# A projection of 512 tokens: one matmul of 512 columns into one PSUM bank instead of two of 256 into two

## The chip, the cores and the metric

The kernel runs on one core of one Trainium2 chip. The metric is the device time of one execution in microseconds; three executions of the kernel before took 2807.52, 2808.34 and 2809.0 us, so the median is 2808.34 us. The profile below is a fourth execution of the same program, recorded with the hardware profiler.

## The reference

The program computes two blocks one after the other on a sequence of 512 tokens with 1024 features, batch 1. The change lies in block 1, which has two layers of one form. Its 16 meta tokens are put ahead of the 512, so it works on 528. Everything is 32-bit.

```python
def hybrid_layer(x, ...):                       # block 1: run twice
    h = rms_norm(x, norm_g)
    z = h @ w_in
    aq, ak, av, ag, mq, mk, mv, mi, mf, mo, mgate = jnp.split(z, split_points(), axis=-1)
    q, k = rope(rms_norm(aq)), rope(rms_norm(ak))          # 16 query heads, 2 key heads of 64
    ya = sliding_window_sink_attention(q, k, av, sink) * silu(ag)
    mq, mk = silu(causal_depthwise_conv([mq, mk]))
    hm = rms_norm(mlstm_chunkwise(mq, mk, mv, mi, mf))     # 4 heads, value width 256
    ym = hm * sigmoid(mo) * silu(mgate)
    return x + jnp.concatenate([ya, ym], -1) @ w_out

def first_block(x, meta, ...):
    h = jnp.concatenate([meta, x], axis=1)
    for l in range(2):
        h = hybrid_layer(h, ...)
    return h[:, 16:]                            # the meta tokens' own output is dropped
```

Block 2 (differential, dilated and memory attention, two layers, then a norm) follows on the 512 tokens. As the meta rows are dropped at the end of block 1, its last layer needs queries (`aq`) and gates (`ag`, `mo`, `mgate`) for 512 tokens only; keys, values and the convolution inputs are needed for all 528.

## The kernel before

Activations lie with features on the 128 partitions and tokens along the free dimension. Every 32-bit operand is split into a rounded high part and a low part (`split`, L167: ScalarE casts the high part at L171, VectorE subtracts for the low part at L172), and each product is three matmuls: high times high, high times low, low times high. So a projection of 128 output features (`dense`, L195) is 24 matmuls over the eight feature tiles for each token range in `halves`, with a weight load ahead of every matmul. All matmuls are issued at L165. A weight chunk of 128x1024 comes by DMA and is itself split into `wh` and `wl` (`weights`, L177).

PSUM has two pools: `z` tiles of two banks, two of them, for the projections, and `a` tiles of one bank, four of them, for everything else. A projection in layer 0 covers 528 tokens as two ranges of 264 (`HALVES`), one in each bank of a `z` tile, and VectorE copies it out times the norm factor in one instruction (`evac1`, L352). In the last layer of block 1, 32 projections (8 of queries, 8 of attention gates, 16 of mLSTM gates) take the 512 tokens alone, as two ranges of 256 (`SEQ2`, chosen at L803 as `own`).

The layer's work is emitted in the order of `ORDER`: attention group 0, mLSTM head 0, attention group 1, and so on. Between projections, generators of the attention blocks (`a_block`, L462) and mLSTM heads (`m_head`, L651) are advanced by one step each (`step`, `round`). One attention block, for four heads and 128 queries, goes through the engines like this: TensorE computes two score tiles, VectorE adds the mask and takes the maximum of each head (L481), three small VectorE operations make the bias (L486 to L489), ScalarE takes four exponentials (L493), VectorE forms the sums and normalises (L497 to L501), TensorE transposes the result (L509), ScalarE and VectorE split it (L171, L172), and TensorE multiplies it with the values (L165, into an `a` tile of 128x4x112).

The order in which an engine's instructions finally stand is not that of the source: the program is laid out by a planner that runs it through its own estimate of durations, emits what is ready, and prefers older work, with the copies out of PSUM raised in rank (`high_priority`). Each engine then executes its list strictly in that order and waits on semaphores. So a change of one instruction's estimated duration moves others on all engines.

Of the kernel before, what the change touches and what calls it, by code (L numbers as in the profile page):

```python
# [13 lines left out]
ALU = mybir.AluOpType  # L14
# [5 lines left out]
L1 = 528  # L20
# [17 lines left out]
FULL = [(0, 512)]  # L38
HALVES = [(0, HB), (HB, L1)]
SEQ1 = [(16, L1)]  # L40
SEQ2 = [(16, 272), (272, L1)]


COL = {}
# [18 lines left out]
class Kernel:  # L63
# [281 lines left out]

    def evac1(self, ps, r, halves=HALVES):
        z = self.slot()
        (t, u), two = halves[0], lambda x: x[:, halves[0][0] :].rearrange("p (a b) -> p a b", a=2)
        if t:
            self.nc.vector.memset(z[:, :t], 0.0)  # L350
        with self.tc.high_priority(offset=AHEAD):
            self.nc.vector.tensor_tensor(two(z), ps[:, :, : u - t], two(r), ALU.mult)  # L352
        return z

    def qk_parts(self, z, gcol):
# [431 lines left out]
    def layer1(self, l, st, xsrc, nxt, first=()):  # L787

        nc, d = self.nc, self.d
        r = self.slot()  # L790
# [9 lines left out]
        self.release(raw)  # L800


        own = SEQ2 if l else HALVES  # L803

        def proj(halves=HALVES):
            ps = self.z()
# [67 lines left out]
        halves = HALVES if l == 0 else SEQ1  # L874
        acc = []
        for part, gens, y in ((0, attn, ya), (1, ml, yb)):
# [7 lines left out]
            for m in range(8):  # L884
                ps = self.z()
                outs = [ps[:, j, : b - a] for j, (a, b) in enumerate(halves)]
                self.dense(outs, [d["wo1"][l, m, part]], ys, halves)
                if part == 0:
                    x = self.slot()
# [720 lines left out]
```

## Time and profile before

| | |
|---|---|
| median of three executions | 2808.34 us (2807.52 to 2809.0) |
| the profiled execution: device time | 2809.2 us |
| the profiled execution: span of its instructions | 2807.4 us |
| TensorE (PE) busy | 2752.0 us, 98% |
| weight loads (PEld, beside PE) | 2439.8 us, 87% |
| VectorE (DVE) busy | 1627.0 us, 58% |
| ScalarE (ACT) busy | 1654.6 us, 59% |
| GpSimd (POOL) busy | 689.8 us, 25% |
| granted TensorE clock, mean | 0.995 |

Busy times are unions: instructions of one engine that overlap are counted once. Matmuls are pipelined, so the duration of a single matmul is longer than the distance from its start to that of the next; the time that a stream of matmuls takes is read from the starts. The span runs from the first to the last instruction; the device time of that execution is 1.8 us longer.

### The profile page before, as it was taken

Reading aid. Unit: us, or ns where it says so; the run is one execution under the profiler, and the core shown is the slowest. Engines: PE = TensorE matmul, PEld = TensorE weight load, DVE = VectorE, ACT = ScalarE, POOL = GpSimd, SP = SyncE. Lnnn points to the kernel's source line nnn. Section 1 sums busy time; section 2 is a strip of 40 time slices with the busy share of each in tenths; the row PEclk is TensorE's granted clock in tenths of the full one; section 3 lists DMA queues with packets and bytes.
Section 4 is the critical chain, followed back from the end, with each engine's and each line's share of the span. In section 5 each row is a group of like instructions: output and inputs, shape, how many; then the busy total and the mean of one; then the engine's idle time right before and its main releaser. Section 6 shows DMA issues by size and latency. Waiting matters only on the chain.

```text
span 2807.4 us, 44298 instructions
## 1 busy us (share of the span) xinstructions
PE 2752.0 (98%) x16806; PEld 2439.8 (87%) x16806; DVE 1627.0 (58%) x4079; ACT 1654.6 (59%) x2926; POOL 689.8 (25%) x790
## 2 busy tenths in 40 slices
PE   8999999999999999999999999999999999999998
PEld 7999999999999878888888888888888888888886
DVE  5788784478777545665445662344676452673333
ACT  6677775677777566777555442236777664553233
POOL 4233222313322322221111211222221121211231
PEclk9999999999999999999999999999999999999999
DMA  7655657766666886756766322347765777422332
GB/s 197 142 129 128 142 133 180 188 138 133 137 142 151 198 204 160 165 126 148 167 147 163 106 76 97 107 136 185 157 150 132 156 163 160 142 78 78 103 120 68
DMA packets 137668, 395.32 MB, mean 141 GB/s; under 512 B 14031, under 2 KB 40343, under 8 KB 137327
## 3 DMA queue, kind: packets, MB, share of 16 engines
q0 software_dynamic: 39456, 143.67, 30.7%
q1 hardware_dynamic: 96846, 247.77, 26.3%
q8 instruction: 132, 2.16, 0.3%
q10 hardware_dynamic: 1152, 1.05, 0.1%
q14 instruction: 82, 0.66, 0.1%
HBM read 383.85 MB, written 8.60 MB: 140 GB/s over the span
## 4 chain that ended last, share of the span: by engine, by line
PE 88%; ACT 6%; DVE 4%; issue 1%; DMA 0%; POOL 0%; DVEq 0%; SPq 0%; ACTq 0%
PE z L165 64%; PE a L165 20%; PE a L967 1%; PE a L509 1%; ACT s L1010 1%; ACT wl L186 1%; ACT wh L188 1%; DVE s L175 1%; DVE s L981 0%; ACT L1038 0%; ACT s L174 0%; DVE s L172 0%; ACT s L171 0%; ACT L229 0%; DMA s<-mem 0%
## 5 line engine op out<-in xcount | busy, mean ns | idle before, releaser
L165 PE MATMUL z<-s,wh 128*128 128x512 f32 (+2 forms) x6784 | 1263.4, 334 | 12.3 <-DVE s L175 3.4
L165 PEld LDWEIGHTS z<-s,wh 128*128 128x128 f32 x6784 | 1042.5, 189 | 143.2 <-DVE s L175 4.6
L165 PE MATMUL z<-s,wl 128*128 128x264 f32 (+2 forms) x3392 | 660.1, 333 | 0.0
L165 PEld LDWEIGHTS z<-s,wl 128*128 128x128 f32 x3392 | 525.7, 188 | 63.1 <-issue 0.5
L187 POOL DMA_DIRECT2D wl<-w x242 | 209.7, 867 | 1060.3 <-ACT wl L186 921.4
L188 ACT CAST wh<-wr 128x1024 fp32r<-128x1024 f32 x274 | 286.7, 1046 | 309.3 <-PE z L165 304.3
L165 PE MATMUL a<-s,s 128*128 128x512 f32 (+5 forms) x1900 | 420.9, 336 | 2.7 <-ACT s L171 1.7
L186 ACT ACTIVATE wl<-wr 128x1024 fp32r<-128x1024 f32 x274 | 288.4, 1056 | 86.3 <-PE z L165 82.9
L165 PEld LDWEIGHTS a<-s,s 128*128 128x128 f32 (+1 forms) x1900 | 295.4, 186 | 33.4 <-ACT s L171 3.3
L190 ACT CAST wh<-wr 128x1024 fp32r<-128x1024 f32 x130 | 136.2, 1049 | 278.3 <-PE z L165 168.7
L192 DVE TENSOR_TENSOR wl<-wr,wh 128x1024 fp32r<-128x1024 f32 x86 | 106.9, 1244 | 199.6 <-ACT wh L190 193.9
L165 PE MATMUL z<-wh,s 128*128 128x256 f32 x1408 | 208.9, 286 | 8.0 <-DVE s L175 7.7
L192 POOL TENSOR_TENSOR wl<-wr,wh 128x1024 fp32r<-128x1024 f32 x44 | 106.3, 2416 | 441.2 <-ACT wh L190 338.6
L172 DVE TENSOR_TENSOR s<-s,s 128x512 fp32r<-128x512 f32 (+7 forms) x266 | 183.8, 704 | 44.1 <-ACT s L171 37.0
L165 PEld LDWEIGHTS z<-wh,s 128*128 128x128 f32 x1408 | 187.7, 191 | 16.5 <-DVE s L175 11.4
L172 DVE TENSOR_TENSOR s<-a,s 128x512 fp32r<-128x512 f32 (+3 forms) x266 | 150.4, 582 | 85.2 <-ACT s L171 84.0
L165 PE MATMUL a<-s,wh 128*128 128x512 f32 (+1 forms) x800 | 189.3, 384 | 0.0
L171 ACT CAST s<-s 128x512 fp32r<-128x512 f32 (+7 forms) x266 | 146.7, 565 | 70.7 <-PE a L165 15.5
L1231 DVE TENSOR_TENSOR s<-z,s 128x512 f32<-128x512 f32 x128 | 87.7, 687 | 168.3 <-PE z L165 153.0
L165 PEld LDWEIGHTS a<-s,wh 128*128 128x128 f32 x800 | 146.0, 188 | 31.9
L171 ACT CAST s<-a 128x512 fp32r<-128x512 f32 (+3 forms) x266 | 126.6, 503 | 62.2 <-PE a L967 33.7
L981 DVE CUSTOM_DVE_ANT_0 s<-a,reg 128x512 f32<-128x512 f32 x160 | 107.9, 686 | 41.2 <-PE a L165 39.6
(263 smaller groups left out, 3197.2 us busy)
## 6 DMA issues: line engine op xcount, KB each, us to landing
wr<-w SPq DMA_DIRECT2D x308, 512.0 KB, 3.5
wl<-w POOLq DMA_DIRECT2D x242, 512.0 KB, 5.9
wr<-wo SPq DMA_DIRECT2D x48, 512.0 KB, 3.6
wl<-wo POOLq DMA_DIRECT2D x32, 512.0 KB, 5.7
wr<-wb SPq DMA_DIRECT2D x32, 512.0 KB, 3.4
reg<-tab SPq DMA_DIRECT2D x24, 448.0 KB
s<-x SPq DMA_DIRECT2D x16, 264.0 KB, 7.3
r<-s SPq DMA_DIRECT2D x16, 256.0 KB, 4.5
```

What stands on the lines that cost most here:

```text
L165: self.nc.tensor.matmul(out, lhsT, rhs, start=start, stop=stop)
L171: nc.scalar.copy(hi, src)
L172: nc.vector.tensor_tensor(lo, src, hi.bitcast(F32), ALU.subtract)
L175: nc.vector.scalar_tensor_tensor(lo, src, scale, hi.bitcast(F32), ALU.mult, ALU.subtract)
L186: nc.scalar.mul(lo, raw, -1.0)
L187: nc.gpsimd.dma_start(lo, src, accum_op=ALU.add)
L188: nc.scalar.copy(hi, raw)
L190: nc.scalar.copy(hi, raw)
L192: (nc.gpsimd if self.nw % 3 == 1 else nc.vector).tensor_tensor(lo, raw, hi.bitcast(F32), ALU.subtract)
L509: nc.tensor.transpose(pt[:, h], sm[h // 2][:, h % 2, 128 * c : 128 * c + 128], self.ident)
L981: self.nc.vector.tensor_tensor_reduce(e, ps, bias[:, 3 - i : 7 - i].rearrange("p a b -> p (a b)"), 1.0, LOW, ALU.add, ALU.max, mx)
L1231: nc.vector.tensor_tensor(z[:, :512], ps, r[:, :512], ALU.mult)
```

## The change

`SEQ2` is dropped, and `own` in the last layer of block 1 becomes `SEQ1`, the one range from token 16 to 528. `dense` then issues 24 matmuls of 512 columns where it issued 48 of 256, all into bank 0 of the `z` tile, with 24 weight loads where there were 48. `evac1` takes the number of ranges from `halves` and reads one bank of 512 instead of two of 256. The `z` tile keeps its two banks, and no DMA is added or removed.

```diff
-SEQ2 = [(16, 272), (272, L1)]
...
     def evac1(self, ps, r, halves=HALVES):
         z = self.slot()
-        (t, u), two = halves[0], lambda x: x[:, halves[0][0] :].rearrange("p (a b) -> p a b", a=2)
+        (t, u), n = halves[0], len(halves)
+        two = lambda x: x[:, t:].rearrange("p (a b) -> p a b", a=n)
         if t:
             self.nc.vector.memset(z[:, :t], 0.0)
         with self.tc.high_priority(offset=AHEAD):
-            self.nc.vector.tensor_tensor(two(z), ps[:, :, : u - t], two(r), ALU.mult)
+            self.nc.vector.tensor_tensor(two(z), ps[:, :n, : u - t], two(r), ALU.mult)
         return z
...
-        own = SEQ2 if l else HALVES
+        own = SEQ1 if l else HALVES
```

The planner's order changes on all engines from the first of these projections to the end of the layer's attention; before and after that stretch the lists are the same but for a few neighbours that swap. Below, rows of an engine's list are shown as they stand: source line, operation, output<-inputs with their numbers, shape, repetitions. The first number of a name is the same in both kernels, the second counts instructions and differs. Lines up to L345 of the changed kernel are one less than before (L164 is the old L165, L170 the old L171, L171 the old L172). `z` tiles are projections, `a` tiles attention.

TensorE in attention group 1, before: from the second pair of scores of the tile a_1559 to the block that follows the transposes a_1564 and a_1567.

```order
L165 MATMUL a_1559_9384<-s_1543_9267,s_1519_9127 128x256 x2
...
L165 MATMUL z_1627_9697<-s_1164_7025,wh_1629_9699 128x264
L509 MATMUL a_1564_9403<-ident_194,s_1535_9243 128x128
...
L509 MATMUL a_1567_9412<-ident_194,s_1536_9244 128x128
L165 MATMUL z_1627_9697<-s_1171_7091,wh_1629_9699 128x264 x2
...
L165 MATMUL z_1648_9824<-s_1150_6893,wh_1650_9826 128x264 x2
L165 MATMUL a_1590_9550<-s_1565_9408,s_1218_7405 128x4x112
L165 MATMUL z_1648_9824<-s_1156_6958,wh_1650_9826 128x264 x2
```

The same place on TensorE in the changed kernel.

```order
L164 MATMUL a_1559_9096<-s_1543_8979,s_1519_8863 128x256 x2
L164 MATMUL z_1648_9536<-s_1177_7156,wl_1651_9539 128x264 x2
L164 MATMUL z_1648_9536<-s_1184_7222,wl_1651_9539 128x264 x2
L509 MATMUL a_1564_9115<-ident_194,s_1535_8955 128x128
...
L509 MATMUL a_1567_9124<-ident_194,s_1536_8956 128x128
L164 MATMUL a_1573_9147<-s_1563_9110,s_1498_8769 128x256 x2
L164 MATMUL a_1574_9154<-s_1563_9110,s_1519_8863 128x256 x2
L164 MATMUL a_1590_9262<-s_1565_9120,s_1218_7405 128x4x112
L164 MATMUL a_1590_9262<-s_1566_9121,s_1218_7405 128x4x112
L164 MATMUL a_1590_9262<-s_1568_9129,s_1218_7405 128x4x112
L164 MATMUL a_1590_9262<-s_1569_9130,s_1218_7405 128x4x112
```

The scores in a_1559 belong to the group's second block; a_1564, a_1567 and a_1590 to its first. Before, 31 projection matmuls of 264 columns stand between the scores and the first transpose, and 38 more between the last transpose and a_1590. In the changed kernel 4 stand before the first transpose, and none between the transposes and a_1590. The next row in the changed kernel is the first matmul of the projection z_1655.

VectorE at that place in the changed kernel: from the mask of a_1559's second head to the copy of the projection z_1627 out of PSUM.

```order
L481 ISA s_1556_9087,t_1557_9088<-a_1559_9096,reg1_192 128x256
...
L295 SCALAR_TENSOR_TENSOR s_1586_9250<-s_1587_9255,s_1586_9250 128x528
L497 TENSOR_TENSOR t_1541_8973<-t_1541_8973,t_1542_8974 128x4
...
L501 TENSOR_SCALAR s_1535_8955<-s_1535_8955,t_1541_8973 128x256 x2
L501 TENSOR_SCALAR s_1536_8956<-s_1536_8956,t_1541_8973 128x256 x2
L488 TENSOR_SCALAR t_1560_9103<-t_1557_9088 128x4
...
L171 TENSOR_TENSOR s_1566_9121<-a_1564_9115,s_1565_9120 128x448
L489 TENSOR_TENSOR t_1577_9163<-cols_100,t_1575_9161 128x4
L171 TENSOR_TENSOR s_1569_9130<-a_1567_9124,s_1568_9129 128x448
L497 TENSOR_TENSOR t_1561_9104<-t_1561_9104,t_1562_9105 128x4
L352 TENSOR_TENSOR s_1631_9465<-z_1627_9409,s_1187_7229 128x528
```

The subtractions that a_1590 reads (s_1566, s_1569) and the copy that frees the bank for z_1655 stand behind the mask of a_1559 here. Of the rows left out, eight are small ones ahead of L488, and between L488 and s_1566 stand four masks (L481), one subtraction of 528 columns and four small ones. On ScalarE the casts of a_1564 and a_1567 stand behind the four exponentials of the block that a_1558 and a_1559 belong to, in both kernels.

TensorE near the end of attention group 3, before: the last transposes of a_2107 and the product a_2110 that uses them.

```order
L509 MATMUL a_2107_12559<-ident_194,s_2069_12375 128x128
L165 MATMUL z_2152_12856<-s_1150_6893,wh_2154_12858 128x256
...
L165 MATMUL z_2152_12856<-s_1184_7222,wl_2155_12859 128x256 x2
L165 MATMUL a_2110_12579<-s_2105_12555,s_1273_7687 128x4x112
L165 MATMUL a_2110_12579<-s_2106_12556,s_1273_7687 128x4x112
L165 MATMUL a_2110_12579<-s_2108_12564,s_1273_7687 128x4x112
```

The same place on TensorE in the changed kernel.

```order
L509 MATMUL a_2104_11878<-ident_194,s_2069_11703 128x128 x2
L509 MATMUL a_2107_11887<-ident_194,s_2069_11703 128x128 x2
L164 MATMUL a_2110_11907<-s_2105_11883,s_1273_7639 128x4x112
L509 MATMUL a_2112_11918<-ident_194,s_2085_11771 128x128 x2
L509 MATMUL a_2112_11918<-ident_194,s_2086_11772 128x128 x2
L164 MATMUL a_2110_11907<-s_2106_11884,s_1273_7639 128x4x112
L164 MATMUL a_2110_11907<-s_2108_11892,s_1273_7639 128x4x112
```

Before, 37 projection matmuls of 256 columns stand between the transposes and a_2110; in the changed kernel none does, and the transposes of the next block are threaded between the four matmuls of a_2110.

## Rows read from the trace of the kernel before

**Rows 1.** The page: busy us, share of span, instructions; shares of the chain
```profile
PE 2752.0 (98%) x16806; PEld 2439.8 (87%) x16806; DVE 1627.0 (58%) x4079; ACT 1654.6 (59%) x2926; POOL 689.8 (25%) x790
...
PE 88%; ACT 6%; DVE 4%; issue 1%; DMA 0%; POOL 0%; DVEq 0%; SPq 0%; ACTq 0%
```

**Rows 2.** Windows: PE, PEld, DVE, ACT, POOL busy (count), clock, DMA share, GB/s
```profile
537.00:909.00 372.00, 371.26 (x3046) 364.44 (x3046) 290.08 (x955) 273.16 (x555) 122.03 (x185) 1.00 0.62 139
60.00:425.00 365.00, 362.78 (x2931) 355.98 (x2931) 289.28 (x951) 267.58 (x562) 113.72 (x159) 1.00 0.61 137
```

**Rows 3.** Groups by shape, PE, 537 to 909: count, busy us, mean ns, idle
```profile
L165 PE MATMUL z<-s,wh 128*128 128x256 f32 x1024 | 140.3, 284 | 0.5 <-DVE s L350 0.5
L165 PE MATMUL z<-s,wl 128*128 128x256 f32 x502 | 72.6, 283 | 0.0
```

**Rows 4.** Timeline of PE, one projection in halves: start, us, form, count
```profile
890.46 3.94 PE L165 MATMUL z<-s,wh 128*128 128x256 f32 x32
894.23 2.05 PE L165 MATMUL z<-s,wl 128*128 128x256 f32 x16
896.13 1.35 PE L165 MATMUL z<-s,wh 128*128 128x256 f32 x10
```

**Rows 5.** Timeline of PE in block 2, one projection of 512 columns
```profile
1704.99 3.89 PE L165 MATMUL z<-s,wh 128*128 128x512 f32 x16
1708.71 2.01 PE L165 MATMUL z<-s,wl 128*128 128x512 f32 x8
1710.56 1.78 PE L165 MATMUL a<-s,wh 128*128 128x512 f32 x7
```

**Rows 6.** Timeline of PE from a_1559's second pair to a_1590
```profile
675.71 0.41 PE L165 MATMUL a<-s,s 128*128 128x256 f32 x2
675.96 1.65 PE L165 MATMUL z<-s,wl 128*128 128x264 f32 x12
...
679.73 0.38 PE L509 MATMUL a<-ident,s 128*128 128x128 f32 x2
...
686.53 0.37 PE L165 MATMUL a<-s,s 128*128 128x448 f32 x1
```

**Rows 7.** Timeline of DVE over the same stretch
```profile
676.16 0.42 DVE L481 CUSTOM_DVE_ANT_0 s<-a,reg 128x256 f32<-128x256 f32 x1
676.51 0.08 DVE L481 DVE_READ_ACCUMULATOR2_ANT t<- 128x1 f32 x1
...
676.72 0.61 DVE L501 TENSOR_SCALAR s<-s,t 128x256 f32<-128x256 f32 x2
677.25 0.70 DVE L296 SCALAR_TENSOR_TENSOR s<-s,s 128x528 f32<-128x528 f32 x1
677.87 0.61 DVE L501 TENSOR_SCALAR s<-s,t 128x256 f32<-128x256 f32 x2
...
684.78 0.58 DVE L172 TENSOR_TENSOR s<-a,s 128x448 fp32r<-128x448 f32 x1
...
687.38 0.69 DVE L352 TENSOR_TENSOR s<-z,s 128x528 f32<-128x528 f32 x1
```

**Rows 8.** Timeline of ACT over the same stretch: exponentials, then casts
```profile
680.01 0.59 ACT L493 ACTIVATE s<-s,t,t 128x256 f32<-128x256 f32 x1
...
682.35 0.19 ACT L496 ACTIVATE t<-t 128x4 f32<-128x4 f32 x1
682.45 0.94 ACT L171 CAST s<-a 128x448 fp32r<-128x448 f32 x2
```

**Rows 9.** Timeline of PE: one long wait, in layer 0
```profile
54.92 0.51 PE L165 MATMUL a<-s,rotr 128*128 128x264 f32 x2 [2.27 <-DVE s L175]
```

**Rows 10.** Windows: behind that wait, and as much time at full clock
```profile
56.00:59.40 3.40, 3.40 (x18) 3.40 (x17) 0.97 (x3) 0.00 (x0) 0.01 (x1) 0.50 0.00 0
437.00:440.40 3.40, 3.40 (x29) 3.37 (x28) 0.00 (x0) 0.00 (x0) 0.08 (x1) 1.00 1.00 219
```

## The prediction

> **What bounds the kernel now.** I read the page first. TensorE is busy for 98% of the span, and 88% of the chain that ended last is its own work [rows 1], so a microsecond taken from or added to its stream is one of the whole. No other engine is above 59% over the span. But a mean over the span hides the stage, so the next view is the windows. In the stretch from 537 to 909 us, where all the changed projections run, TensorE is busy for 371.26 of 372 us: it waits for 0.74 us in all. VectorE is busy there for 290 us, 78%, and ScalarE for 273, 73% [rows 2]. So nothing is left to gain from waits in this stretch, while two engines with three quarters of their time taken feed TensorE through lists of fixed order. The third view, groups by shape, shows the matmuls in question: 1024 and 502 of 256 columns are recorded, of 1536 in the program (32 projections of 48) [rows 3].
>
> The mean of a group, 284 ns, is the latency of one matmul. The rate is read from starts. 48 matmuls of 256 run from 890.46 to 896.13 without a break: 118.1 ns each, 236.3 for a pair [rows 4]. 24 of 512, one projection of block 2, run from 1704.99 to 1710.56: 232.1 ns each [rows 5]. A pair of halves thus costs only 4.2 ns more than the whole: the stream is paid by columns, and the weight load that the second half repeats lies beside the first.
>
> **The change, part by part.** *Fewer matmuls.* 768 pairs become 768 single ones: 768 x 4.2 ns = 3.2 us off TensorE's stream. From the parts of these rows the pair costs 235.6 to 237.5 ns and the single 231.3 to 232.5, so the bounds are 2.4 and 4.8 us. No other work hides this gain, as TensorE does not wait there. *The copy.* One read of 512 in one bank stands for one of twice 256; the 528-column copy takes 0.69 us [rows 7]; the number of elements is the same, and I cost the edit at nothing. If it differed by 0.05 us, 32 of them would be 1.6 us of VectorE, which has 82 us free in the stretch [rows 2].
>
> The Trainium skill, "TensorE: Matmul & The Clock Gate", section "Back-to-back issue gap", gives N/2.4 + 2.5 ns for a matmul by itself, and by that a pair would save 2.5 ns, or 1.9 us in all. The same section states some 131 ns for N=512 in a sustained stream of loads and matmuls, which would make 80 us of it. The trace's streams have 232 ns for 512 columns [rows 5], and so the measurement stands against the second figure.
>
> *The moved instructions.* The larger effect is in the order. In the changed lists the attention's matmuls come in bunches with few projection matmuls between. At most places a block's product stands further behind its transposes than before; at a few it stands nearer, and at two of these no projection matmul is left between.
>
> Place A is the one around a_1559 in attention group 1. Count from the start of a_1559's second pair. TensorE's own work up to the first matmul of z_1655 is: that pair 0.25 us (675.71 to 675.96 [rows 6]), 4 projection matmuls at 0.12, 8 transposes at some 0.11 (two take 0.38 with the last one's latency [rows 6]), 8 score matmuls at 0.12 and 4 products of 448 columns at 0.2 (both by columns from rows 4): 0.25 + 0.5 + 0.9 + 1.0 + 0.8 = 3.45 us. The other engines need longer. VectorE begins the mask of this pair 0.45 us after its start (676.16 less 675.71 [rows 6, 7]). Up to L488 it then has, back to back, a mask 0.35 (676.16 to 676.51), a product of 528 columns 0.62 (677.25 to 677.87), four normalisations 1.05 (0.53 for two, 676.72 to 677.25) and nine small ones that I put at 0.12 each, an estimate (the one shown takes 0.08 [rows 7], a small one of ScalarE 0.19 [rows 8]): 3.1 us, so 3.55 has passed. ScalarE's four exponentials take 2.34 (680.01 to 682.35) and the two casts 0.94 [rows 8]: 6.85. Meanwhile VectorE does four masks, a subtraction and small ones, some 2.5 us, so it is free at 6.1 and starts the second subtraction when its cast is there: 0.58 [rows 7], 7.45. One small one and the copy of z_1627, 0.69 [rows 7], end at 8.25. Only then has z_1655 a bank, and TensorE reached it at 3.45. It loses **4.8 us**, part of it already at a_1564, which needs the normalised block, and at a_1590. Before, some 70 projection matmuls lay over this chain, and it took 9.65 us from 675.71 to the second subtraction's end at 685.36 without a wait [rows 6, 7]. Bounds: if every engine served this chain alone, 0.45 + 0.35 + 0.35 + 2.34 + 0.94 + 0.58 = 5.0 against TensorE's 3.25 up to the last product, 1.75 us lost; with the delays of before, 9.65 less 3.25, 6.4 us. I take 4.8, since it goes by the changed list.
>
> *The clock.* After the wait of 2.27 us at 54.92 [rows 9] the granted clock was 0.50 (1.2 instead of 2.4 GHz) for 3.4 us, with 18 matmuls of this width done, against 29 in as much time at 1.00 [rows 10]. The 11 missing ones at 0.117 us are 1.3 us. Place A idles longer than that, so I add **1.3 us**; bounds 0 and 2.6 (the fall twice).
>
> *Place B* is a_2110 in group 3. Its first product comes right after the transposes. The cast of a_2104 can start some 0.05 us after the last of the row's transposes has started (its latency is 0.27, the 0.38 of two less 0.11 [rows 6]; the two of a_2107 behind it take 0.22) and takes 0.47 [rows 8], so about **0.5 us** is lost; the later three are covered by the eight transposes threaded in. Without any cover it would be cast, cast and subtraction, 1.5 us.
>
> *Elsewhere.* Layer 0 runs the same code, planned in yet another order, and TensorE idles there for 2.2 us of 365 [rows 2], 1.5 more than in the last layer. I take half of that, **0.7 us**, for other new waits, between 0 and 1.5.
>
> **The sum**, against the profiled execution (span 2807.4, device time 2809.2): -3.2 + 4.8 + 1.3 + 0.5 + 0.7 = +4.1, so 2813.3; the median of the runs shown is 0.86 us below that execution, so the forecast is 2808.34 + 4.1 = 2812.4 us. The bounds add to -3.0 from all lows (-4.8 + 1.75) and +10 from all highs.
>
> **Rivals.** *The gain comes through.* The planner may have placed a_1564 early because VectorE is in truth ahead, and the chain of A may be over when TensorE arrives. The time would be 2808.34 - 3.2 = 2805.1, faster. For it: the planner's order of before left 0.74 us of waits [rows 2]. Against it: the distance between the pair and what needs it is 3.45 us of work, and even the chain alone needs 5.0. It decides if the first subtraction of a_1564 ends within 3.3 us of the pair's start. *A short wait.* The chain alone binds at A, and the clock does not fall: -3.2 + 1.75, and 0.4 for a part of B, make -1.1: 2807.3. *More meetings like A.* In bunched stretches VectorE, at 78% already [rows 2], becomes the bound, and copies are late at one or two further places, with waits that sum to a second A and its clock: 4.1 + 4.8 + 1.3 = +10.2, 2818.5. For it: group 3 must make up there what it was put off, in a shorter time. *Weight loads set the pace.* If the 256-wide stream were held by its loads, whose group is busy for 364 of 372 us [rows 2], a single one could run well under 232 ns and the change would save 10 us or more: 2798. Against it: the 512-wide stream of block 2, with half the loads per column, has the same rate [rows 5].
>
> **How the numbers follow.** Forecast 0.48; the gain comes through 0.19; a short wait 0.17; more meetings 0.13; loads 0.03. A difference under 0.2%, 5.6 us, is about what a measurement of this kernel can tell from no change: 2802.7 to 2814.0. The forecast's own spread, 2810 to 2816, puts 0.18 above that line and 0.30 within. So slower 0.18 + 0.13 = 0.31; same 0.30 + 0.16 + 0.17 = 0.63, where 0.03 of the first rival lies beyond the faster bound; faster 0.03 + 0.03 = 0.06. The range, 2804.5 to 2818.5, takes in both near rivals and most of the third.
>
> **What would show it.** In the profile after: 768 matmuls of 512 columns more, at about 232 ns from start to start in an unbroken projection; TensorE's idle time in the stretch grown from 0.7 to 6 or 7 us; in its list of waits, VectorE's normalisation (L501), subtraction (L171) or copy (L352) near 685 to 695 us, several microseconds together; a granted clock of 0.50 right behind. It is wrong if TensorE stays without waits there (the time is then 2805), if waits of A's size are found at other places instead, or if the pitch of the 512-wide matmuls in this layer is not that of block 2, for instance because the attention's matmuls in between cost something at each switch.

## The result, and the profile after

The changed kernel takes 2821.92 us in the median of four runs (2820.71 to 2824.08), the kernel before 2807.93 us in the median of four (2802.79 to 2809.0). The ratio is 1.0054, with a 95% interval of 1.0042 to 1.0067: the change makes the kernel slower by 14 us. The forecast was 2812.4 us, with a range that ended at 2818.5.

The page of the changed kernel, the lines that answer to [rows 1]:

```profile
PE 2755.6 (98%) x16038; PEld 2401.0 (85%) x16038; DVE 1625.0 (58%) x4079; ACT 1655.3 (59%) x2926; POOL 687.2 (24%) x790
...
PE 85%; DVE 7%; ACT 6%; issue 1%; DMA 1%; POOL 0%; DVEq 0%; ACTq 0%; SPq 0%
```

768 matmuls are gone (16806 to 16038). Of the chain that ended last, VectorE has 7% where it had 4%: that is where to look. The next view is one window, called the layer below: from the first changed projection to one and the same matmul of the layer's output, behind the last attention and mLSTM work of TensorE. For the kernel before:

```profile
536.90:971.80 434.90, 433.19 (x3347) 415.13 (x3346) 320.35 (x1028) 308.55 (x619) 140.10 (x203) 1.00 0.65 148
```

and for the same work in the changed kernel:

```profile
533.50:983.50 450.00, 438.53 (x2580) 378.42 (x2578) 318.53 (x1028) 309.09 (x619) 137.75 (x203) 0.99 0.63 143
```

The layer takes 450.0 us for 434.9, TensorE is idle in it for 11.5 us for 1.7, and VectorE and ScalarE have nearly the same work as before. The groups by shape in the changed layer (compare [rows 3]) show the new form, 512 and 255 recorded of 768, and no longer the 256-wide one:

```profile
L164 PE MATMUL z<-s,wh 128*128 128x512 f32 x512 | 131.4, 400 | 1.3 <-DVE s L352 1.2
...
L164 PE MATMUL z<-s,wl 128*128 128x512 f32 x255 | 70.2, 398 | 0.0
```

The means are latencies again. The rate is read from the starts in TensorE's timeline, one projection in an unbroken run:

```profile
637.90 3.88 PE L164 MATMUL z<-s,wh 128*128 128x512 f32 x16
641.61 0.39 PE L164 MATMUL z<-s,wl 128*128 128x512 f32 x1
```

16 matmuls lie between these two starts: 231.9 ns each, as in block 2 [rows 5]. The figure of some 131 ns that the Trainium skill states ("TensorE: Matmul & The Clock Gate", section "Back-to-back issue gap") is not seen in this layer either.

What TensorE waited for in the layer's stretch 537 to 935 us, the longest entries (engine, line waited for; total, times, longest):

```profile
PE a L164 <- ACT s L170: 1.6, 2, 0.8
PE a L164 <- DVE s L526: 1.6, 2, 1.1
PE a L164 <- DVE s L171: 1.6, 4, 0.6
PE a L509 <- DVE s L501: 1.4, 1, 1.4
PE z L164 <- DVE s L352: 1.2, 3, 0.8
PE a L663 <- DVE s L526: 1.1, 1, 1.1
PE a L164 <- DVE t L481: 1.0, 2, 0.7
```

Most are instructions of attention blocks on VectorE and ScalarE. The prediction had named L501, L171 and L352 near 685 to 695 us; the waits are not all at place A, and L526 and L481 were not among those named. By the code these two read an `a` tile, and the scores and transposes that wait for them do not read what they write: there TensorE waits for a bank of the `a` pool, 3.7 us of the list. Place A itself, on TensorE (compare [rows 6]):

```profile
685.00 0.41 PE L164 MATMUL a<-s,s 128*128 128x256 f32 x2
685.25 0.66 PE L164 MATMUL z<-s,wl 128*128 128x264 f32 x4
687.33 0.44 PE L509 MATMUL a<-ident,s 128*128 128x128 f32 x2 [1.43 <-DVE s L501]
687.52 0.72 PE L164 MATMUL a<-s,s 128*128 128x256 f32 x4
688.08 1.11 PE L509 MATMUL a<-ident,s 128*128 128x128 f32 x6
689.16 0.51 PE L164 MATMUL a<-s,s 128*128 128x256 f32 x2
690.41 0.51 PE L164 MATMUL a<-s,s 128*128 128x256 f32 x2 [0.74 <-DVE t L481]
691.72 0.47 PE L164 MATMUL a<-s,s 128*128 128x448 f32 x1 [0.81 <-ACT s L170]
692.56 1.07 PE L164 MATMUL a<-s,s 128*128 128x448 f32 x3 [0.37 <-DVE s L171]
693.85 2.50 PE L164 MATMUL z<-s,wh 128*128 128x512 f32 x5 [0.22 <-DVE s L352]
```

From the pair of a_1559 (685.00) to the first matmul of z_1655 (693.85) 8.85 us pass; 8.25 had been worked out. On VectorE, the three releasers in the order forecast (compare [rows 7]); the first normalisation ends just before the first transpose starts, the first subtraction just before the second product, and the copy just before z_1655:

```profile
686.93 0.35 DVE L501 TENSOR_SCALAR s<-s,t 128x256 f32<-128x256 f32 x1
...
687.19 1.51 DVE L501 TENSOR_SCALAR s<-s,t 128x256 f32<-128x256 f32 x3
...
691.89 0.62 DVE L171 TENSOR_TENSOR s<-a,s 128x448 fp32r<-128x448 f32 x1
...
692.49 0.62 DVE L171 TENSOR_TENSOR s<-a,s 128x448 fp32r<-128x448 f32 x1
...
693.10 0.70 DVE L352 TENSOR_TENSOR s<-z,s 128x528 f32<-128x528 f32 x1
```

On ScalarE, the casts that the first product waits for (compare [rows 8]):

```profile
691.16 0.94 ACT L170 CAST s<-a 128x448 fp32r<-128x448 f32 x2
```

Right behind place A the granted clock falls to half, 1.2 instead of 2.4 GHz (window as in [rows 10]):

```profile
693.50:696.90 3.40, 3.18 (x8) 2.47 (x8) 3.26 (x14) 1.67 (x6) 0.00 (x0) 0.50 0.70 135
```

The trace's starts give the price: from 693.85 to the start of the ninth at 697.20, eight matmuls of 512 columns take 3.35 us, and at 232 ns each they would take 1.86: 1.5 us lost.

To compare kernels I sum TensorE's starts over the layer. Each start-to-start distance is split into the usual one of its shape (4 ns and 0.445 ns a column, which fits the 118 and 232 ns of [rows 4, 5]; 109 for a transpose), what a stretch at clock 0.50 adds, waits of more than 0.13 us, and small gaps. A wait counted in this way comes out some 0.15 us longer than the idle time that the lists show for it, so these sums are larger than those of the lists. All in us:

| kernel | layer | matmuls | waits | low clock | small gaps | median of all |
|---|---|---|---|---|---|---|
| before | 434.9 | 425.9 | 3.2 | 0 | 5.8 | 2807.9 |
| after | 450.0 | 422.9 | 15.9 | 3.2 | 8.0 | 2821.9 |

So the layer loses 15.1 us: 3.0 gained in matmuls, 12.7 lost in waits, 3.2 at the low clock, 2.2 in small gaps. The waits by place, times of the changed kernel (x2 to x4 are experiments, below):

| place (us) | before | after | x2 | x3 | x4 |
|---|---|---|---|---|---|
| 572 | 0.4 | 0.9 | 0.6 | 0.6 | 1.0 |
| 599 to 603 | 0.7 | 1.5 | 1.5 | 0.7 | 1.5 |
| 685 to 697, place A | 0 | 5.0 | 4.9 | 0 | 5.2 |
| 787 to 799, group 2 | 0 | 1.7 | 1.7 | 1.8 | 0 |
| 884 to 897, group 3 | 0.1 | 3.0 | 2.9 | 3.0 | 0.1 |
| 910, place B | 0 | 1.0 | 1.0 | 1.1 | 0 |
| 922 to 929, layer's end | 1.7 | 2.9 | 3.4 | 3.9 | 1.8 |

Outside the layer the two profiled executions differ by falls of the clock that come and go (last section): before 537 us the one of the kernel before had two and the other none (3.4 us, with the same lists there), and behind the layer the changed one had a fall at 1024.6 us more (1.5 us). 15.1 - 3.4 + 1.5 - 0.6 for the rest is the 12.6 between the spans.

### The profile page after: what moved, and what is told of

Read it like the earlier page. It is cut to its first block, busy times and chain, and to the rows that moved or that the text cites. A ratio compares the mean times of both kernels' runs of the same rounds, so it can differ in the third digit from the quotient of the medians.

```text
span 2820.0 us, 42763 instructions
## 1 busy us (share of the span) xinstructions
PE 2755.6 (98%) x16038; PEld 2401.0 (85%) x16038; DVE 1625.0 (58%) x4079; ACT 1655.3 (59%) x2926; POOL 687.2 (24%) x790
## 4 chain that ended last, share of the span: by engine, by line
PE 85%; DVE 7%; ACT 6%; issue 1%; DMA 1%; POOL 0%; DVEq 0%; ACTq 0%; SPq 0%
PE z L164 62%; PE a L164 20%; PE a L967 1%; PE a L509 1%; DVE s L171 1%; ACT s L1010 1%; ACT wl L185 1%; ACT wh L187 1%; DVE s L174 1%; DVE s L981 0%; ACT L1038 0%; ACT s L170 0%; ACT s L173 0%; ACT L228 0%; DVE s L295 0%
## 5 line engine op out<-in xcount | busy, mean ns | idle before, releaser
L164 PE MATMUL z<-s,wh 128*128 128x512 f32 (+2 forms) x6272 | 1252.2, 347 | 12.5 <-DVE s L174 3.7
L164 PEld LDWEIGHTS z<-s,wh 128*128 128x128 f32 x6272 | 1006.1, 189 | 163.7 <-DVE s L174 4.8
L164 PE MATMUL z<-s,wl 128*128 128x512 f32 (+2 forms) x3136 | 656.1, 346 | 0.0
L164 PEld LDWEIGHTS z<-s,wl 128*128 128x128 f32 x3136 | 505.9, 188 | 72.3 <-issue 0.5
L164 PE MATMUL a<-s,s 128*128 128x512 f32 (+5 forms) x1900 | 421.7, 338 | 8.5 <-ACT s L170 3.3
L185 ACT ACTIVATE wl<-wr 128x1024 fp32r<-128x1024 f32 x274 | 288.5, 1056 | 88.7 <-PE z L164 85.2
L164 PEld LDWEIGHTS a<-s,s 128*128 128x128 f32 (+1 forms) x1900 | 296.9, 187 | 46.2 <-ACT s L170 6.0
L164 PE MATMUL z<-wh,s 128*128 128x256 f32 x1408 | 208.8, 286 | 7.7 <-DVE s L174 7.5
L171 DVE TENSOR_TENSOR s<-s,s 128x512 fp32r<-128x512 f32 (+7 forms) x266 | 185.7, 711 | 47.8 <-ACT s L170 38.5
L164 PEld LDWEIGHTS z<-wh,s 128*128 128x128 f32 x1408 | 187.5, 191 | 16.4 <-DVE s L174 11.1
L171 DVE TENSOR_TENSOR s<-a,s 128x512 fp32r<-128x512 f32 (+3 forms) x266 | 150.2, 583 | 85.2 <-ACT s L170 83.6
L164 PE MATMUL a<-s,wh 128*128 128x512 f32 (+1 forms) x800 | 189.3, 384 | 0.0
L170 ACT CAST s<-s 128x512 fp32r<-128x512 f32 (+7 forms) x266 | 146.7, 566 | 70.4 <-PE a L164 16.1
L164 PEld LDWEIGHTS a<-s,wh 128*128 128x128 f32 x800 | 146.0, 188 | 31.9
L170 ACT CAST s<-a 128x512 fp32r<-128x512 f32 (+3 forms) x266 | 126.4, 503 | 59.7 <-PE a L967 33.7
```

The source lines that it names most:

```text
L164: self.nc.tensor.matmul(out, lhsT, rhs, start=start, stop=stop)
L170: nc.scalar.copy(hi, src)
L171: nc.vector.tensor_tensor(lo, src, hi.bitcast(F32), ALU.subtract)
L185: nc.scalar.mul(lo, raw, -1.0)
```

## The experiments

Theory "order": the time was lost by where the planner put the instructions, not by the operand. The rivals: the single operand in one bank costs by itself ("operand"), or VectorE, at 78%, sets a sum of waits that only moves about ("VectorE is the bound").

**Operand and order crossed.** For these runs each engine's list can be held in the order that was planned for another form of the kernel: the other form is traced first, and then every instruction is tied behind the one that stands before it in that list. Such an edge sets the order alone, with no wait. x1 is the changed kernel in the order of the kernel before, x2 the reverse.

```diff
+                for order, stop in plans:
+                    for e, n in order:
...
+                        for i in (ins[e][n], second.get((e, n))):
+                            if i is not None:
+                                if e in last:
+                                    tc.add_manual_dep(i, last[e], nosync, reason="order")
+                                last[e] = i.name
...
+    _, b = trace(SEQ2)
+    nc, _ = trace(SEQ1, [(b, None)])
```

> The 32 projections take their 512 tokens as one moving operand, but every engine's list is held in the order of the kernel before. Theory 'order' (the waits come from where the planner put the instructions): the waits of the changed kernel are gone, TensorE waits for 0.7 to 2 us between 537 and 910 us, no fall of the granted clock in the layer, and the 3.1 us of fewer matmuls remain: 2807.9 - 3.1 = 2805 us. Rival 'operand' (a single operand in one bank makes copies or banks late by itself): the waits are back at the same projections and the time is 2816 to 2822 us.

Measured: 2805.45 us, ratio to before 0.9993 (0.9984 to 1.0001). The layer takes 431.5 us, 3.4 less than before, with 3.8 us of waits. All that TensorE waits for in it, 2.1 us as idle time:

```profile
PE a L167 <- DVE s L174: 0.6, 1, 0.6
PE z L167 <- DVE s L355: 0.5, 1, 0.5
PE a L595 <- DVE t L593: 0.5, 1, 0.5
PE a L167 <- ACT s L689: 0.3, 1, 0.3
PE z L167 <- DVE s L357: 0.2, 1, 0.2
```

and the window of this layer, with VectorE's 320.66 us of work as before:

```profile
534.20:965.70 431.50, 429.39 (x2578) 374.97 (x2578) 320.66 (x1028) 308.26 (x619) 139.95 (x203) 1.00 0.65 149
```

> The 32 projections are computed in two halves in two banks as before, but every engine's list is held in the order of the changed kernel, the second half right behind the first. Theory 'order': the waits near 685 to 695 us, in group 2, in group 3 and at the layer's end are there without the change of operand, and the time is 2821.9 + 3.1 = 2825 us, 2821 to 2826. Rival 'operand': the time is that of the kernel before, 2808 us.

Measured: 2827.69 us, ratio 1.0067 (1.0054 to 1.008), somewhat more than expected; its profile has two falls of the clock before 537 us. The layer takes 453.6 us, 3.6 more than the changed kernel's, with the same 15.9 us of waits at the same places (table). TensorE at A, now with halves:

```profile
691.77 0.44 PE L514 MATMUL a<-ident,s 128*128 128x128 f32 x2 [1.43 <-DVE s L506]
...
694.85 0.51 PE L167 MATMUL a<-s,s 128*128 128x256 f32 x2 [0.74 <-DVE t L486]
696.17 0.47 PE L167 MATMUL a<-s,s 128*128 128x448 f32 x1 [0.81 <-ACT s L173]
697.00 1.15 PE L167 MATMUL a<-s,s 128*128 128x448 f32 x3 [0.36 <-DVE s L174]
```

1.43, 0.74, 0.81, 0.36: the waits of the changed kernel to 0.01 us. The order makes them, and the operand is worth 3.4 to 3.6 us of the layer in the other direction. "Operand" falls.

**Half of the order.** The lists are joined at a matmul of group 1's last block (a_1619 in the old list, a_1618 in the new one), behind place A. x3 has the old order before it and the new one behind, x4 the reverse; both have one operand.

```diff
+    nc, _ = trace(SEQ1, [(b, ("EngineType.PE", 5033)), (a, None)])
```

```diff
+    nc, _ = trace(SEQ1, [(a, ("EngineType.PE", 5030)), (b, None)])
```

> One operand of 512 tokens; the lists follow the kernel before up to the end of attention group 1, and the changed kernel from there on. Theory 'order', with waits that stand each for itself: the waits at 572, 599 and 685 to 697 us of the changed kernel (0.6 + 0.8 more than before, 5.0, and 1.5 of the lower clock) are gone, the others stay: 2821.9 - 7.9 = 2814 us. Rival 'VectorE is the bound' (what is saved in group 1 is paid in groups 2 and 3): 2818 to 2822 us, with more than 8 us of waits behind 780 us.

Measured: 2816.75 us, ratio 1.0034 (1.0022 to 1.0046). The layer takes 441.0 us, 9.0 less than the changed kernel's where 7.9 were expected; the median is 2.8 us above the expectation. The waits up to 697 us are gone, those behind 780 us stand as they were, except 1.0 us more at the layer's end, behind which the clock does not fall here. This run alone does not tell the theories apart: its median lies between the two expectations, and the rival's mark, more than 8 us of waits behind 780 us, was no test, since the changed kernel has 8.6 there itself and x3 9.8. The reverse tells more.

> One operand of 512 tokens; the lists follow the changed kernel up to the end of attention group 1, and the kernel before from there on. Theory 'order', with waits that stand each for itself: only the waits up to 697 us stay, 7.9 us with the lower clock behind place A, and 3.1 us of fewer matmuls are gained: 2807.9 + 7.9 - 3.1 = 2812.7 us. Rival 'VectorE is the bound': new waits in groups 2 and 3 in spite of the old order there, 2816 us or more. If place A alone were the whole cost, 2822 us.

Measured: 2812.91 us, ratio 1.0018 (1.0009 to 1.0027), with 441.5 us for the layer. Only the early waits are left, and one of 1.5 us just behind the joint. The losses of the two halves, 441.0 and 441.5 against 431.5 for the old order, are 9.5 and 10.0 us; together 19.5, and the whole new order loses 18.5. But for the 1.0 us at the end of x3, each place stands for itself: what is saved at one is not paid at another, as it would be if VectorE were the bound, and x4 has none of the new waits in groups 2 and 3 that this rival asked for.

**Cover at A.** (Cover is the work of TensorE that stands between an instruction and what it waits for.) In the changed kernel's lists 19 matmuls of z_1655 are moved ahead, between the transposes, scores and product of A, and the copy of z_1627, which frees their bank, 31 rows ahead on VectorE. As it stands the copy cannot go earlier than a_1590: it writes the SBUF slot of s_1565, an operand of that product. So it gets a slot that is idle then.

```diff
+    z = out(PE, "z_1655")
+    move(z[:7], out(PE, "a_1564")[0])
+    move(z[7:11], out(PE, "a_1573")[2])
+    move(z[11:19], out(PE, "a_1590")[0])
+    (copy,) = src(DVE, "z_1627")
+    dve = [k for k in a if k[0] == DVE]
+    move([copy], dve[dve.index(out(DVE, "s_1586")[-1]) - 3])
+    MOVED["s_1631"] = "s56"
+    nc, _, _ = trace(SEQ1, [(a, None)])
```

> The changed kernel with its lists held, except at place A: 19 of the 24 matmuls of the projection z_1655 (4.4 us) stand between the transposes, scores and product at which TensorE waits there; for that the copy of z_1627 stands 31 rows earlier on VectorE, and takes an SBUF slot that is idle at that time. Theory 'order' (A costs what TensorE lacks in cover): A's waits fall from 5.0 to about 1 us, the granted clock does not fall behind it (1.5 us), all other places stay: 2821.9 - 5.5 = 2816.5 us, 2815 to 2819. Rival 'VectorE is the bound' (the chain of VectorE and ScalarE sets the pace, and cover only moves the wait): waits of 4 us or more at the next transposes, 2820 to 2822 us.

Measured: 2819.27 us, ratio 1.004 (1.0027 to 1.0052); this is between what "order" (2815 to 2819) and "VectorE is the bound" (2820 to 2822) expected. TensorE at A:

```profile
687.15 1.78 PE L169 MATMUL z<-s,wh 128*128 128x512 f32 x7
688.77 0.41 PE L516 MATMUL a<-ident,s 128*128 128x128 f32 x2
...
690.36 1.17 PE L169 MATMUL z<-s,wh 128*128 128x512 f32 x4
...
692.16 1.32 PE L169 MATMUL z<-s,wh 128*128 128x512 f32 x5
...
695.25 1.55 PE L516 MATMUL a<-ident,s 128*128 128x128 f32 x8 [0.20 <-DVE s L508]
...
697.90 0.47 PE L169 MATMUL a<-s,s 128*128 128x256 f32 x2 [0.86 <-DVE s L533]
```

The old waits are filled, and no fall of the clock follows. But about half of them come back behind it, where the next block now has none of the matmuls that were moved: 2.6 us are left of 5.0. The layer gains 3.5 us. Both theories have a part here: cover decides whether TensorE waits, and within ten microseconds VectorE's chain can still be the limit.

**Parts of the change**, each with an order of the planner's own: only the queries, only the attention gates, or only the mLSTM gates take one operand. The edit for the queries alone:

```diff
         own = SEQ1 if l else HALVES
+        gown = SEQ2 if l else HALVES
+        mown = SEQ2 if l else HALVES
...
-                gs.append(gate())
+                gs.append(gate(gown))
...
-                zo = self.evac1(proj(own), r, own)
+                zo = self.evac1(proj(mown), r, mown)
```

> Only the 8 query projections take one operand; the planner orders anew. Theory 'order': 0.8 us of matmuls is gained, and the planner's new order has waits of its own that do not follow from the share of the change: 2807.9 - 0.8 plus what TensorE waits beyond before's 3 us and what the clock costs after it; anything from 2806 to 2825. Rival 'operand' (a single operand costs by itself): a quarter of 14 us, 2811.4 us, with the waits at the queries.

> Only the 8 gate projections of attention take one operand; the planner orders anew. Theory 'order': 0.8 us of matmuls is gained, and the waits follow the new order, not the share: 2806 to 2825 us. Rival 'operand': a quarter of 14 us, 2811.4 us, with the waits at these gates.

> Only the 16 gate projections of the mLSTM heads take one operand; the planner orders anew. Theory 'order': 1.5 us of matmuls is gained, and the waits follow the new order, not the share: 2805 to 2825 us. Rival 'operand': half of 14 us, 2814.9 us, with the waits at these gates.

| kernel | median | ratio to before | layer | waits | low clock |
|---|---|---|---|---|---|
| x6, queries | 2805.5 | 0.9992 (0.9983 to 1.0000) | 433.8 | 3.0 | 0 |
| x7, attention gates | 2811.3 | 1.0014 (1.0005 to 1.0023) | 439.3 | 6.1 | 1.6 |
| x8, mLSTM gates | 2814.7 | 1.0027 (1.0018 to 1.0036) | 440.9 | 8.4 | 1.5 |

The totals of x7 and x8 are those that "operand" expected, by chance: x6 is not, and x1, x2 and x12 rule it out. The expectation of "order" here was so wide that these runs alone could not have failed it. The places settle it: x8 has 1.0 us at 691, 2.6 at 890 to 895 and 3.2 at the layer's end, and its longest wait, 1.7 us, is for a small copy in an mLSTM head's values (L667), not for a gate's copy.

**Attention earlier.** In the last layer each projection advances attention by 2.5 rounds instead of 2; x9 with one operand, x10 with halves, x11 with one operand in x10's order.

```diff
+        ra = (2.5, 1) if l else RA
...
-                self.step(*RA)
+                self.step(*ra)
```

> The changed kernel (one operand), but in the last layer each projection advances attention by 2.5 rounds instead of 2, so that attention is written earlier in the program; the planner orders anew. By its list, 2 of the 20 attention products have less than 1.4 us of TensorE work between their transposes and themselves (the kernel before has 2, the changed kernel 6). Theory 'order': 2 to 4 us of waits in the layer as before, and the 3.1 us of fewer matmuls: 2802 to 2808 us. Rival 'VectorE is the bound': the waits are set by VectorE's 78%, not by places, and come to 10 us or more in this order too: 2814 us or more.

> The kernel before (two halves in two banks) with the same 2.5 rounds in the last layer. 2 of 20 products have less than 1.4 us of cover. Theory 'order': within 3 us of the kernel before, 2805 to 2811 us, which shows what a new order alone does. Rival 'operand' (halves are what avoids the waits): 2805 to 2808 us here and 2815 or more with one operand.

> One operand, with the lists held in the order that the planner gives the two halves at 2.5 rounds. Theory 'order': 3 us below the run with the halves in that order (2802 to 2808 us), with the same waits at the same places. Rival 'operand': 2815 us or more.

Measured: 2847.45, 2835.27 and 2832.45 us; ratios 1.0146 (1.0131 to 1.0161), 1.0103 (1.0086 to 1.0119) and 1.009 (1.0075 to 1.0105). All totals are far off, since some 25 us are lost behind the layer, in block 2, in all three. The first stretch of block 2 in x10:

```profile
1092.00:1400.00 308.00, 293.80 (x1556) 247.31 (x1555) 179.85 (x425) 209.07 (x345) 60.62 (x71) 0.99 0.63 146
```

and the same stretch in the kernel before:

```profile
1092.00:1400.00 308.00, 301.36 (x1612) 255.85 (x1612) 181.83 (x427) 214.43 (x356) 63.41 (x73) 0.99 0.67 151
```

TensorE is idle for 14.2 us of the 308, and was for 6.6. The likely reason is that the counter of due rounds leaves the layer with half a round more, and block 2, at 1.5 rounds a step, runs in another phase; this was not tried apart. The layer alone can still be compared: 449.5, 436.4 and 433.0 us, with 14.9, 4.7 and 5.2 us of waits. x11 is 2.8 us faster than x10 and its layer 3.4: the third time that the operand alone is worth this. And x9 refutes my count: only 2 of its 20 products have less than 1.4 us of cover, yet it waits as the changed kernel does. The distance from transposes to product is not enough to tell; of its two longest waits, 2.0 us each, one is for L501 ahead of transposes (599 us) and one for L666, a copy in an mLSTM head, at the layer's end. In its waits x9 is also where "VectorE is the bound" had put it (10 us or more). What speaks against that is x11: the same work in x10's order, with 319.4 us of it on VectorE in the layer for x9's 321.1, waits 5.2 us.

**Both together.** One operand everywhere, in the order of x6.

```diff
+    _, b, _ = trace((SEQ1, SEQ2, SEQ2))
+    nc, _, _ = trace((SEQ1, SEQ1, SEQ1), [(b, None)])
```

> All 32 projections take one operand, with the lists held in the order that the planner made when only the queries did (the run that was fastest so far with an order of the planner's own). Theory 'order': the layer's waits are those of that run, 3.0 us, and 2.3 us of matmuls more are gained: 2805.5 - 2.3 = 2803 us, 2802 to 2806. Rival 'operand': the gates' single operands bring their waits back, 2812 us or more.

Measured: 2803.26 us (11 runs), ratio 0.9984 (0.9975 to 0.9993): faster than both kernels, 18.7 us below the changed one. The layer takes 431.2 us with 3.3 us of waits. So the edit is a gain when the order is right.

## Why the prediction was wrong, step by step

- *Fewer matmuls* (-3.2 us): right. 3.0 by counts and pitch in the layer, and 3.4 to 3.6 between kernels of one order (x1, x2, x11).
- *The copy* (0): right. The 512-wide copy takes 684 ns in both kernels.
- *Place A* (4.8): right in place, chain and size: 5.0 us, 8.85 us from the pair to z_1655 where 8.25 were worked out. One wait on the way, 0.74 us for an `a` bank that L481 had to read, was not in the chain.
- *The clock* (1.3): right at A, 1.5. A second fall at the layer's end, 1.7, had no term.
- *Place B* (0.5, up to 1.5): 1.0, for the cast as said, but at twice the size. TensorE there, the eight transposes and the first product behind them:

```profile
909.33 1.03 PE L509 MATMUL a<-ident,s 128*128 128x128 f32 x8
911.20 0.47 PE L164 MATMUL a<-s,s 128*128 128x448 f32 x1 [0.83 <-ACT s L170]
```

and ScalarE, on which an instruction for the low part of a weight chunk (L185), itself held up by TensorE for 0.81 us, stands ahead of the casts. The transposes have ended at 910.36, and the prediction let the cast start with them; it starts at 910.62, when that instruction is done:

```profile
909.53 1.06 ACT L185 ACTIVATE wl<-wr 128x1024 fp32r<-128x1024 f32 x1 [0.81 <-PE z L164]
910.62 0.97 ACT L170 CAST s<-a 128x448 fp32r<-128x448 f32 x2
```

- *Elsewhere* (0.7, 0 to 1.5): this is the step that failed. The waits beyond before's come to 12.7 us in the layer; less A and B, 6.7 are elsewhere, in all the other rows of the table; with 2.2 in small gaps and 1.7 of the second fall it is 10.6 where 0.7 stood. The term was taken from layer 0, as if its 2.2 us of idle time bounded what another order can cost. Layer 0 is one order among many. The changed list was there to be followed through, as it was at A and B: two scores of the next block directly behind eight transposes, with a wait behind them, stand at 798 and 894 us as well:

```profile
891.95 1.03 PE L509 MATMUL a<-ident,s 128*128 128x128 f32 x8
892.74 0.48 PE L164 MATMUL a<-s,s 128*128 128x256 f32 x2
894.36 0.87 PE L164 MATMUL a<-s,s 128*128 128x256 f32 x4 [1.14 <-DVE s L526]
```

I followed the two places with the shortest distance and took the rest to be small. And I counted operands and the `z` bank alone: of 7.0 us of idle time at the other places, 3.0 are waits for VectorE to empty an `a` bank (L526 and L481).

The sum of the layer is thus -3.0 + 5.0 + 1.5 + 1.0 + 10.6 = 15.1 us for the +4.1 forecast. The highs of the five terms, as stated, add to +9.6 ("+10"), and the median moved by +14. Of the rivals, *more meetings like A* came nearest: waits at further places that sum to more than a second A, and a second fall of the clock. Its price, 2818.5, was 3.4 us too low. Its reason does not hold: VectorE has as much work in x1 and x12, where TensorE hardly waits. The other three are ruled out by the waits at A and the pitch of 231.9 ns.

What stays open is why the planner makes a worse list from the single operands. It did so in both full pairs (15.9 against 3.2 us of waits, and 14.9 against 4.7 at 2.5 rounds), and with 8, 8 and 16 of the 32 it came to 3.0, 6.1 and 8.4. That looks like more than chance, but no run here tells what in its plan does it.

## What to carry over

Where a planner sets the order, an edit has two effects: what it does to the instructions, and a new order. Price them apart, by holding one of the two; here they were -3.4 and +18.5 us in the layer. And when one place in the new list shows a wait, follow the whole list before giving the rest a small number: the places add up one by one.

## What the runs showed of the chip

The same code at the start of the program meets a fall of the granted clock to 0.50 at about 15 and 55 us in some executions and not in others. Of the 14 profiles five had both, and the layer began at 536.9 to 538.2 us; six had one, and it began at 533.7 to 536.6; three had none, and it began at 531.9 to 534.2. A fall behind the layer (near 1024 us) came in eight of the 14, and the same stretch of work there (from the end of the window to some 1092 us in the kernel before) was 121.9 us long with it and 120.4 without. Nor did similar waits always bring a fall: at the layer's end the clock fell at 920.4 us in x8, behind waits of 1.9 and 0.4 us, and in x3 waits of 1.3, 1.0, 0.4 and 0.6 us between 918 and 922 us brought none. So a difference of 2 to 4 us between two single executions of this kernel says nothing; the layer's own time from the trace told the kernels apart much better than the totals did.
